# An own list scheduler orders all engines of a two-layer diffusion backbone, in place of the framework's order with hints

## The chip, the core and the metric

The kernel runs on one NeuronCore of a Trainium2 chip: TensorE (PE, matrix products), VectorE (DVE), ScalarE (ACT), GpSimd (POOL) and SyncE (SP), which issues most of the DMAs. Each engine works through its own list of instructions in order and waits on semaphores for the others. The metric is the device time of one execution in microseconds (us), the median of several.

## The reference, cut to what matters

The input is 256 latent tokens (`x`) and 256 context tokens (`ctx`), 1024 wide; there are two layers. All arithmetic is float32.

```python
for layer in range(2):
    mx = silu(c) @ w_ada[layer] + b_ada[layer]          # nine shift/scale/gate vectors, latent
    mc = silu(c_ctx) @ w_ada[layer] + b_ada[layer]      # the same for the context
    x  = x + 0.5 * mx[2] * swiglu(pre_norm(x, nw[0], mx, 0), ffn_up[layer, 0], ffn_down[layer, 0])
    ...                                                 # the context likewise
    yc, yx = token_mix(pre_norm(xc, ...), pre_norm(x, ...), ...)
    x  = x + mx[5] * yx
    x  = x + 0.5 * mx[8] * swiglu(pre_norm(x, nw[2], mx, 2), ffn_up[layer, 1], ffn_down[layer, 1])
return rms_norm(x, final_norm)
```

`pre_norm` is an RMS norm with a shift and a scale per channel. `swiglu` is 1024 to 2 x 2816 to 1024. `token_mix` projects the normalised tokens once (`w_in`), runs four bidirectional mixers (gated DeltaNet, Hyena, Mamba-2 SSD, gated linear attention) over chunks of 64 tokens, gates and merges them, and projects back (`w_out`).

## The kernel before, in words

**Dense work.** Activations lie transposed, 128 channels by 512 tokens a tile. A weight matrix comes in chunks of 128x1024 floats (512 KB): SP loads one into a `raw` tile (three buffers), POOL rounds it to fp32r (`wh`, L248; in part of the mixers ACT does, L245), DVE subtracts for the rest (`wl`, L249; or POOL, L246). PE takes three matmuls per tile to get float32 accuracy: `wh` x `hh` (L294), `wl` x `hh` (L295), `wh` x `hl` (L296); in the start L401 to L403 do this, for a projection by tokens L791 to L793. `wh` and `wl` have three buffers each, so a split waits until PE has done with the chunk three before.

**Norms.** `rstd_tok` sums squares on PE (L608), DVE makes the reciprocal root in a chain of eleven tiny instructions (`ms` L611, then `rq`, `rt`, `ru`, L210 to L215), PE broadcasts it (L623), DVE multiplies (`u`, L632), ACT and POOL apply scale and shift (`hh` L657, `v` L658), DVE takes the difference (`hl`, L659).

**adaLN vectors.** `ada` (from L508) multiplies `w_ada` by the condition on DVE in 1024 instructions (`aa`, L528 and L530) on loads `aw` of 256 KB. `pump` strews them under the dense work of the FFNs. The two vectors that the first norm needs are made on PE in `start` (L377).

**Mixers.** `weave` (L1964) runs two generators against each other: `chain`, the recurrent work of the mixers (many small instructions that go back and forth between PE, DVE, ACT and POOL, such as the triangular inverse `XA`, `Y`, `A` at L1092 to L1120), and `dense`, the projections. Tuned numbers (`PACE`) set how they interleave.

**What sets the order.** `start` is emitted under `manual_schedule`, so it runs in the order of the source; `norm_G` does this for PE. All the rest is ordered by the framework's scheduler, which is steered by hints: `issue_after` (a split or a load may not go before a named instruction; `gate`, `last_ld`), `high_priority` (weight splits get an offset), and the interleaving above. Tiles of one tag rotate through its buffers.

## Time and profile before

| what | value |
|---|---|
| median of 3 runs | 2842.53 us (2841.36 to 2853.82) |
| the profiled execution | 2847.14 us |
| its span, first to last instruction | 2845.2 us |
| PE busy | 2689.9 us, 95% |
| DVE, POOL, ACT busy | 2036.7 (72%), 1038.9 (37%), 529.4 us (19%) |
| mean granted TensorE clock | 0.978 of full speed |
| DMA | 382.66 MB, mean 134 GB/s |

The profiled execution is 4.6 us above the median; 1.9 us of it lie outside the span. The program goes through these stretches: start and first part of the first FFN (0 to 72 us), rest of that FFN (to 468), mixers of layer 0 (to 1209), output projection, second FFN and first FFN of layer 1 (to 2060), mixers of layer 1 (to 2634), last FFN for the latent tokens alone and output.

### The profile page before, as it was taken

The page shows a single profiled execution, that of the slowest core. Times are in us where ns is not written, and L with a number is a line of the kernel's source. Part 1 is how long each engine was busy: PE and PEld are TensorE (multiplying, and loading weights), DVE is VectorE, ACT ScalarE, POOL GpSimd, SP SyncE. Part 2 cuts the span into 40 slices and gives each one's busy share as a digit, 9 for nine tenths or more (in the row PEclk, how much of TensorE's full clock was granted, in tenths as well). Part 3 has the DMA queues.
Part 4 walks back from the last instruction along what each step waited for, and adds up shares of the span by engine and source line. Part 5 has one row for each costly group of instructions (what it writes and reads, how often), then busy time and mean ns, then how long its engine had stood idle before and what let it go on. Part 6 is the DMA issues. An engine that isn't in the chain of part 4 may idle for free. (4 is left out here: it accounts for less than half of the span.)

```text
span 2845.2 us, 40232 instructions
## 1 busy us (share of the span) xinstructions
PE 2689.9 (95%) x15131; PEld 2289.9 (80%) x15131; DVE 2036.7 (72%) x3763; ACT 529.4 (19%) x1044; POOL 1038.9 (37%) x1007
## 2 busy tenths in 40 slices
PE   7999999989999999999999999999987899989998
PEld 5777767778888878877778877788877798889998
DVE  5999875699575564459965469966479877778656
ACT  2000012533224231111000020000042322311100
POOL 4333313221332554535322233322244233455443
PEclk8999999999999999999999999999999999999999
DMA  9556534322434233234644336543333344445554
GB/s 273 168 178 198 174 109 132 89 75 71 141 112 131 77 100 101 85 116 145 180 145 130 102 110 181 176 146 117 95 89 108 96 138 133 143 150 186 154 185 142
DMA packets 369697, 382.66 MB, mean 134 GB/s; under 512 B 43466, under 2 KB 317544, under 8 KB 369504
## 3 DMA queue, kind: packets, MB, share of 16 engines
q1 hardware_dynamic: 347568, 363.67, 42.7%
q10 hardware_dynamic: 21936, 16.44, 1.8%
q8 instruction: 119, 1.95, 0.3%
q14 instruction: 74, 0.61, 0.1%
HBM read 355.79 MB, written 24.25 MB: 134 GB/s over the span
## 5 line engine op out<-in xcount | busy, mean ns | idle before, releaser
L248 POOL TENSOR_SCALAR wh<-raw 128x1024 fp32r<-128x1024 f32 (+1 forms) x460 | 570.7, 1241 | 1181.7 <-PE pmm L296 716.5
L294 PE MATMUL pmm<-hh,wh 128*128 128x512 f32 (+1 forms) x2432 | 887.0, 365 | 14.8 <-ACT raw L964 8.7
L295 PE MATMUL pmm<-hh,wl 128*128 128x512 f32 (+1 forms) x2432 | 880.7, 362 | 18.8 <-DVE wl L249 18.8
L296 PE MATMUL pmm<-hl,wh 128*128 128x512 f32 (+1 forms) x2432 | 878.8, 362 | 6.3 <-DVE hl L659 6.3
L249 DVE TENSOR_TENSOR wl<-raw,wh 128x1024 fp32r<-128x1024 f32 (+1 forms) x460 | 581.8, 1266 | 388.4 <-POOL wh L248 387.7
L295 PEld LDWEIGHTS pmm<-hh,wl 128*128 128x128 f32 x2432 | 467.6, 192 | 91.1 <-DVE wl L249 26.1
L294 PEld LDWEIGHTS pmm<-hh,wh 128*128 128x128 f32 x2432 | 467.5, 192 | 86.7 <-issue 15.4
L296 PEld LDWEIGHTS pmm<-hl,wh 128*128 128x128 f32 x2432 | 467.0, 192 | 76.2 <-DVE hl L659 10.6
L530 DVE SCALAR_TENSOR_TENSOR aa<-aw,cond,aa 128x256 f32<-128x256 f32 x896 | 423.9, 534 | 0.5 <-DMA aw<-in_w_ada 0.5
L295 PE MATMUL pmm<-ah,wl 128*128 128x512 f32 (+1 forms) x704 | 256.6, 364 | 1.6 <-DVE wl L249 1.4
L294 PE MATMUL pmm<-ah,wh 128*128 128x512 f32 (+1 forms) x704 | 258.0, 366 | 0.0
L296 PE MATMUL pmm<-al,wh 128*128 128x512 f32 (+1 forms) x704 | 256.5, 364 | 0.0
L682 ACT ACTIVATE sil<-pmm 128x512 f32<-128x512 f32 (+1 forms) x88 | 48.0, 545 | 812.2 <-PE pmm L296 773.3
L257 POOL TENSOR_SCALAR ah<-sil 128x512 fp32r<-128x512 f32 (+1 forms) x88 | 71.5, 813 | 251.5 <-DVE sil L687 228.8
L295 PEld LDWEIGHTS pmm<-ah,wl 128*128 128x128 f32 x704 | 133.2, 189 | 23.9 <-DVE wl L249 3.3
L294 PEld LDWEIGHTS pmm<-ah,wh 128*128 128x128 f32 x704 | 133.3, 189 | 23.2 <-issue 2.0
L296 PEld LDWEIGHTS pmm<-al,wh 128*128 128x128 f32 x704 | 133.3, 189 | 21.5 <-issue 0.8
L793 PE MATMUL pmm<-wl,hh 128*128 128x256 f32 x416 | 120.1, 289 | 6.3 <-DVE wl L249 6.3
L791 PE MATMUL pmm<-wh,hh 128*128 128x256 f32 x416 | 120.8, 290 | 0.0
L792 PE MATMUL pmm<-wh,hl 128*128 128x256 f32 x416 | 119.6, 288 | 0.0
L260 DVE TENSOR_TENSOR al<-sil,ah 128x512 fp32r<-128x512 f32 (+1 forms) x88 | 93.0, 1057 | 18.4 <-POOL ah L257 18.4
L296 PE MATMUL pmm<-yl,wh 128*128 128x512 f32 (+1 forms) x256 | 86.5, 338 | 1.3 <-DVE yl L260 1.3
(435 smaller groups left out, 3667.3 us busy)
## 6 DMA issues: line engine op xcount, KB each, us to landing
raw<-in_ffn_up SPq DMA_DIRECT2D x172, 512.0 KB
raw<-in_w_in SPq DMA_DIRECT2D x164, 512.0 KB
aw<-in_w_ada SPq DMA_DIRECT2D x288, 256.0 KB
raw<-in_ffn_down SPq DMA_DIRECT2D x80, 512.0 KB
raw<-in_w_branch SPq DMA_DIRECT2D x32, 512.0 KB
fe<-pk SPq DMA_DIRECT2D x42, 256.0 KB
raw<-in_w_out SPq DMA_DIRECT2D x16, 512.0 KB
pk<-pj ACTq DMA_DIRECT2D x26, 256.0 KB
```

Source lines behind the costliest of these rows:

```text
L248: nc.gpsimd.tensor_scalar(h, r, 1.0, 1.0, op0=ALU.mult, op1=ALU.mult)
L249: nc.vector.tensor_tensor(l, r, h.bitcast(F32), op=ALU.subtract)
L257: nc.gpsimd.tensor_scalar(hi, x, 1.0, 1.0, op0=ALU.mult, op1=ALU.mult)
L260: nc.vector.tensor_tensor(lo, x, hi.bitcast(F32), op=ALU.subtract)
L294: nc.tensor.matmul(o, h[:, k, js], rh[:, tj:t1], start=st, stop=False)
L295: nc.tensor.matmul(o, l[:, k, js], rh[:, tj:t1], start=False, stop=False)
L296: self.last_mm = nc.tensor.matmul(o, h[:, k, js], rl[:, tj:t1], start=False, stop=sp)
L530: nc.vector.scalar_tensor_tensor(a, x, c, a, op0=ALU.mult, op1=ALU.add)
L682: self.last_act = nc.scalar.activation(s[:, t0:t1], ps, AF.Silu)
L791: nc.tensor.matmul(o, rh[:, ts], h[:, k, :], start=st, stop=False, skip_group_check=True)
L792: nc.tensor.matmul(o, rl[:, ts], h[:, k, :], start=False, stop=False, skip_group_check=True)
L793: self.last_mm = nc.tensor.matmul(o, rh[:, ts], l[:, k, :], start=False, stop=sp, skip_group_check=True)
```

## The change

The body of the kernel is left as it is, but it is first run on a stand-in (`Stand`) which only notes each instruction: its engine, operands, the instructions that it depends on (by the overlap of rectangles of a tile, `box`), a cost by formulas (`cost`), and a key, which is the PE time noted so far. `Plan` then places all instructions of the five engines, SP's loads included, by a greedy simulation: whenever an engine is free, it takes of its ready instructions the one with the lowest key. An instruction counts as ready 150 ns (`margin`) and a latency after an instruction of another engine that it needs. Each tag's buffers are given out in the same pass. `build` emits the real instructions in that order under `manual_schedule` for all engines, each buffer as a tile of its own. The hints `issue_after`, `high_priority` and `manual_schedule` do nothing on the stand-in. Two tags get a buffer more (`adas` 1 to 2, `rows` 2 to 3). The instructions themselves stay the same, but for ACT's table loads, 31 before and 36 now.

```diff
+class Stand:
...
+    @contextlib.contextmanager
+    def issue_after(self, ins):
+        yield
...
+    def box(self, ap):
+        off, dims = ap.offset, list(ap.ap)
+        row = int(np.prod(self.tiles[ap.tensor.name][3][1:]))
+        p0, f0 = off // row, off % row
+        lo = hi = f0
+        for s, n in dims[1:]:
+            if s < 0:
+                lo += s * (n - 1)
+            else:
+                hi += s * (n - 1)
+        return p0, p0 + dims[0][1], lo, hi + 1
...
+        self.cost(o, aps)
+        o.key = self.t - self.off[-1]
+        if eng == "PE":
+            self.t += o.occ / 1e3
...
+    def cost(self, o, aps):
...
+        if o.dma:
+            o.occ, o.dur = (60.0 if o.eng == "SP" else 600.0), None
...
+            o.dur = 4.0 * n
+            return
...
+        elif o.eng == "DVE":
+            if o.name in ("tensor_scalar", "tensor_copy", "memset") and not ps and not r:
+                o.dur = 190 + 0.6 * E if o.name != "memset" else 100 + 0.5 * E
+            elif o.name == "scalar_tensor_tensor":
+                o.dur = max(150 + 1.045 * E, 250 + 0.87 * E) if E > 32 else 165
...
+            else:
+                o.dur = 150 + 1.06 * E
+            o.occ = o.dur - 70
...
+class Plan:
+    LAT = {"PE": 60, "DVE": 60, "ACT": 60, "POOL": 90, "SP": 90}
...
+                if e == "ACT":
+                    ta = table_of(o)
+                    if ta and ta != table:
+                        k += self.swap
+                if best is None or k < best[0]:
+                    best = k, n, c
...
+            if o.dma:
+                b = max(t + occ, dmaf)
+                dmaf = b + dur / 230.0
+                end = dmaf + 2300
+            else:
+                end = t + dur
...
+                elif x.eng == e and not o.dma:
+                    r = end if e != "PE" else t + occ
+                else:
+                    r = end + self.LAT[x.eng] + self.margin
...
+def build(nc, tc, es, st, plan):
...
+        return pools[pn].tile(list(shape), dtype, name=tn, tag=f"{tag}_{plan.slot[tn]}", bufs=1)
...
+    for n in plan.seq:
+        o = st.ops[n]
...
+        getattr(engines[o.eng], o.name)(*[sub(a) for a in o.args], **{k: sub(v) for k, v in o.kw.items()})
...
-            s = self.pt.tile([128, 256], F32, name=self.nm("adas"), tag="adas", bufs=1)
+            s = self.pt.tile([128, 256], F32, name=self.nm("adas"), tag="adas", bufs=2)
...
-        t = self.pt.tile([128, 128], F32, name=self.nm("rows"), tag="rows", bufs=2)
+        t = self.pt.tile([128, 128], F32, name=self.nm("rows"), tag="rows", bufs=3)
...
+def order(st):
+    plan = Plan(st, {}, 150.0, 8.0)
...
-    with _tile.TileContext(nc) as tc:
-        body(nc, tc, I, O)
+    st = Stand(nc)
+    body(st, st, I, O)
+    plan = order(st)
+    with _tile.TileContext(nc) as tc, contextlib.ExitStack() as es:
+        with tc.manual_schedule(engines=set(ENGINES)):
+            build(nc, tc, es, st, plan)
```

**The order at three places.** The number behind a tile's name is counted anew by each program; the first number (`raw22`, `ms52`) is the same in both. In the changed kernel every instruction has the line of `build` (L567).

Place 1, the start. On SP, the first loads after the inputs, before: `raw` are the first up-projection weights (a first and a second half, x2), `aw18` to `aw111` the `w_ada` blocks of the first norm, `aw153` onward those of the later vectors, `Fm` and `win` constants of the Hyena filter.

```order
L348 DMA aw21_131<-in_w_ada 128x4x128
L348 DMA raw22_136<-in_ffn_up 128x2x256 x2
L348 DMA aw23_139<-in_w_ada 128x4x128
...
L348 DMA raw31_155<-in_ffn_up 128x2x256 x2
L348 DMA raw71_338<-in_ffn_up 128x2x256 x2
L1641 DMA Fm0_1109<-in_dftF 128x512
...
L348 DMA aw63_322<-in_w_ada 128x4x128
...
L2012 DMA grp_80<-in_grp 128x10
L2013 DMA cmats_79<-in_cmats 128x9x128
...
L516 DMA aw153_789<-in_w_ada 128x512
```

And now:

```order
L567 DMA aw21_102<-in_w_ada 128x4x128
...
L567 DMA aw30_120<-in_w_ada 128x4x128
L567 DMA raw22_126<-in_ffn_up 128x2x256
L567 DMA raw31_128<-in_ffn_up 128x2x256
...
L567 DMA raw71_146<-in_ffn_up 128x2x256
L567 DMA grp_149<-in_grp 128x10
L567 DMA cmats_98<-in_cmats 128x9x128
L567 DMA aw153_152<-in_w_ada 128x512
...
L567 DMA aw170_161<-in_w_ada 128x512
L567 DMA Fm0_166<-in_dftF 128x512
...
L567 DMA aw70_264<-in_w_ada 128x4x128
...
L567 DMA raw22_126<-in_ffn_up 128x2x256
L567 DMA raw31_128<-in_ffn_up 128x2x256
L567 DMA raw71_146<-in_ffn_up 128x2x256
```

The second halves of the three first weight chunks have moved from right behind the first halves to behind `cmats`, five later `w_ada` blocks and the filter's constants. DVE, at the first norm, before (`ms` to `rq` is the root, `u` the product):

```order
L339 TENSOR_TENSOR acc32_159<-acc32_159,sq42_204 128x512
L339 TENSOR_TENSOR acc32_159<-acc32_159,sq46_222 128x512
L611 TENSOR_SCALAR ms52_263<-px51_254 128x4
L210 TENSOR_SCALAR rq53_265<-ms52_263 128x4
L213 TENSOR_TENSOR rt54_266<-ms52_263,rq53_265 128x4
...
L215 SCALAR_TENSOR_TENSOR rq53_265<-ru55_268,rq53_265 128x4
L389 TENSOR_REDUCE c00_299<-px49_235 128x4
...
L632 TENSOR_TENSOR u59_308<-x1_85,px58_303 128x512
L632 TENSOR_TENSOR u60_310<-x2_86,px58_303 128x512
L368 TENSOR_TENSOR wl62_313<-raw22_136,wh61_312 128x1024
```

And now:

```order
L567 COPY x7_286<-px45_278 128x512
L567 TENSOR_TENSOR acc32_242<-acc32_242,sq46_299 128x512
L567 COPY cond17_80<-cond2_320 128x8x2
L567 TENSOR_SCALAR aa157_331<-aw153_152,cond2_320 128x256
...
L567 SCALAR_TENSOR_TENSOR aa157_331<-aw155_156,cond2_320,aa157_331 128x256
...
L567 SCALAR_TENSOR_TENSOR aa163_362<-aw156_159,cond2_320,aa163_362 128x256
L567 TENSOR_SCALAR ms52_417<-px51_324 128x4
L567 SCALAR_TENSOR_TENSOR aa160_369<-aw156_159,cond2_320,aa160_369 128x256
L567 TENSOR_SCALAR rq53_424<-ms52_417 128x4
...
L567 SCALAR_TENSOR_TENSOR aa162_347<-aw170_161,cond2_320,aa162_347 128x256
L567 TENSOR_TENSOR wl62_493<-raw22_126,wh61_462 128x1024
L567 TENSOR_TENSOR u59_508<-x1_233,px58_489 128x512
```

Sixteen `aa` on `aw153` to `aw156`, which stood behind the whole start, now stand ahead of or between the first links of the root (14 of them ahead), and `wl62`, which needs the second half of `raw22`, ahead of the first `u`.

Place 2, the norm before the second FFN of layer 0 (`norm_G(0, 2)`), on DVE, before:

```order
L249 TENSOR_TENSOR wl2210_11287<-raw2208_11284,wh2209_11286 128x1024
L611 TENSOR_SCALAR ms2148_11083<-px2147_11074 128x4
L210 TENSOR_SCALAR rq2149_11085<-ms2148_11083 128x4
L213 TENSOR_TENSOR rt2150_11086<-ms2148_11083,rq2149_11085 128x4
L214 SCALAR_TENSOR_TENSOR ru2151_11088<-rt2150_11086,rq2149_11085 128x4
L1706 COPY gn2153_11101<-px2152_11098 1x256
L215 SCALAR_TENSOR_TENSOR rq2149_11085<-ru2151_11088,rq2149_11085 128x4
...
L214 SCALAR_TENSOR_TENSOR ru2151_11088<-rt2150_11086,rq2149_11085 128x4
L215 SCALAR_TENSOR_TENSOR rq2149_11085<-ru2151_11088,rq2149_11085 128x4
L1710 MEMSET gB2145_11064 1x256
L632 TENSOR_TENSOR u2156_11117<-x2092_10774,px2155_11112 128x512
```

And now:

```order
L567 TENSOR_SCALAR ms2148_11301<-px2147_11279 128x4
L567 SCALAR_TENSOR_TENSOR aa2314_11200<-aw2334_11202,cond2_320,aa2314_11200 128x256
L567 TENSOR_SCALAR rq2149_11308<-ms2148_11301 128x4
L567 SCALAR_TENSOR_TENSOR aa2318_11205<-aw2334_11202,cond2_320,aa2318_11205 128x256
L567 TENSOR_TENSOR rt2150_11312<-ms2148_11301,rq2149_11308 128x4
L567 COPY gn2153_11314<-px2152_11297 1x256
L567 SCALAR_TENSOR_TENSOR ru2151_11317<-rt2150_11312,rq2149_11308 128x4
L567 SCALAR_TENSOR_TENSOR aa2315_11208<-aw2334_11202,cond2_320,aa2315_11208 128x256
...
L567 SCALAR_TENSOR_TENSOR ru2151_11317<-rt2150_11312,rq2149_11308 128x4
L567 SCALAR_TENSOR_TENSOR aa2321_11228<-aw2335_11219,cond2_320,aa2321_11228 128x256
L567 SCALAR_TENSOR_TENSOR rq2149_11308<-ru2151_11317,rq2149_11308 128x4
L567 SCALAR_TENSOR_TENSOR aa2314_11200<-aw2347_11234,cond2_320,aa2314_11200 128x256
L567 SCALAR_TENSOR_TENSOR aa2318_11205<-aw2347_11234,cond2_320,aa2318_11205 128x256
```

Eight `aa` now stand between the eleven links of the chain, and five more between its end and the first `u`.

Place 3, the triangular inverse of the gated DeltaNet in layer 0, on PE, before (`px1031` is the first product of the inverse, `pmm` are dense):

```order
L296 MATMUL pmm1074_5479<-hl777_4098,wh1071_5462 128x512
L294 MATMUL pmm1073_5466<-hh780_4107,wh1088_5559 128x512
L1104 MATMUL px1031_5229<-XA1025_5198,MC902_4628 128x128 x4
L295 MATMUL pmm1073_5466<-hh780_4107,wl1089_5560 128x512
L296 MATMUL pmm1073_5466<-hl781_4108,wh1088_5559 128x512
```

And now:

```order
L567 MATMUL pmm1074_5344<-hl777_4224,wh1071_5219 128x512
L567 MATMUL pmm1073_5321<-hh780_4207,wh1088_5323 128x512
L567 MATMUL pmm1073_5321<-hh780_4207,wl1089_5334 128x512
...
L567 MATMUL pmm1074_5344<-hh786_4234,wl1089_5334 128x512
L567 MATMUL pmm1074_5344<-hl787_4256,wh1088_5323 128x512
L567 MATMUL px1031_5408<-XA1025_317,MC902_4715 128x128 x4
L567 MATMUL pmm1074_5344<-hh789_4245,wh1088_5323 128x512
L567 MATMUL pmm1074_5344<-hh789_4245,wl1089_5334 128x512
L567 MATMUL px1048_5426<-XA1042_3964,MC912_4774 128x128 x4
```

The first product stood behind one dense matmul of the chunk `wh1088` and now stands behind 21. Its producer on DVE, before (`XA1025` is its operand, `qkv` a convolution):

```order
L249 TENSOR_TENSOR wl1089_5560<-raw1087_5557,wh1088_5559 128x1024
L887 SCALAR_TENSOR_TENSOR qkv1016_5155<-raw1017_5156,vB0_3279,qkv1016_5155 128x2x254
L887 SCALAR_TENSOR_TENSOR qkv1018_5176<-raw1019_5177,vB0_3279,qkv1018_5176 128x2x254
...
L887 SCALAR_TENSOR_TENSOR qkv1018_5176<-raw1019_5177,vB0_3279,qkv1018_5176 128x2x254
L1079 STREAM_TRANSPOSE X0T1022_5191<-X01020_5187 128x512
L1080 STREAM_TRANSPOSE X11023_5192<-X1T1021_5188 128x512
L1082 TENSOR_TENSOR XC1024_5195<-X0T1022_5191,X1T1021_5188 128x512
L1092 COPY XA1025_5198<-X01020_5187 32x4x32
L1083 TENSOR_TENSOR XC1024_5195<-XC1024_5195,cmats_79 128x512
L1092 COPY XA1025_5198<-X01020_5187 32x4x32
```

And now:

```order
L567 TENSOR_TENSOR X939_262<-X939_262,P1012_5300 128x31
L567 SCALAR_TENSOR_TENSOR qkv1018_5302<-raw1019_5224,vB0_1399,qkv1018_5302 128x2x254
L567 SCALAR_TENSOR_TENSOR qkv1018_5302<-raw1019_5224,vB0_1399,qkv1018_5302 128x2x255 x2
L567 SCALAR_TENSOR_TENSOR qkv1018_5302<-raw1019_5224,vB0_1399,qkv1018_5302 128x2x254
L567 TENSOR_TENSOR wl1089_5334<-raw1087_5198,wh1088_5323 128x1024
L567 COPY XA1025_317<-X01020_5340 32x4x32 x2
L567 COPY A81027_406<-X01020_5340 32x4x32
L567 STREAM_TRANSPOSE X0T1022_5372<-X01020_5340 128x512
```

The copies of `XA1025` have moved ahead of the transposes and of `XC`, and no convolution stands between them and `wl1089` any more: four stand just ahead of `wl1089`, four further ahead.

## Rows read from the trace of the kernel before

**Rows 1.** Page, part 1: busy us, share of the span, instructions.

```profile
PE 2689.9 (95%) x15131; PEld 2289.9 (80%) x15131; DVE 2036.7 (72%) x3763; ACT 529.4 (19%) x1044; POOL 1038.9 (37%) x1007
```

**Rows 2.** Windows, six stretches: us, engines' busy us, granted clock, DMA share, GB/s.

```profile
0.00:72.00 72.00, 54.24 (x426) 40.86 (x427) 37.19 (x88) 20.41 (x40) 28.53 (x34) 0.83 0.96 271
72.00:468.00 396.00, 381.97 (x1734) 303.86 (x1732) 343.61 (x663) 29.44 (x52) 121.23 (x87) 0.98 0.55 165
468.00:1209.00 741.00, 710.50 (x3978) 605.63 (x3978) 479.82 (x939) 232.37 (x452) 293.41 (x295) 0.99 0.33 98
1209.00:2060.00 851.00, 828.30 (x3726) 669.04 (x3725) 591.98 (x1025) 72.05 (x126) 265.70 (x237) 0.99 0.46 137
2060.00:2634.00 574.00, 516.05 (x3654) 473.06 (x3652) 455.65 (x870) 156.07 (x333) 241.01 (x260) 0.96 0.44 130
2634.00:2845.20 211.20, 198.84 (x1621) 197.44 (x1621) 128.41 (x182) 19.03 (x42) 89.06 (x96) 0.97 0.51 160
```

**Rows 3.** Windows: a full stretch of the mixers, and 8 us behind a wait.

```profile
1067.00:1138.00 71.00, 71.00 (x333) 59.73 (x332) 31.22 (x45) 14.05 (x31) 34.45 (x32) 1.00 0.34 101
613.00:621.00 8.00, 8.00 (x40) 7.49 (x41) 5.40 (x15) 2.66 (x10) 1.93 (x5) 0.65 0.21 66
```

**Rows 4.** Waits of PE: line and releaser, us in total, times, longest us.

```profile
PE pmm L295 <- DVE wl L249: 20.2, 18, 3.2
PE px L1104 <- DVE XA L1092: 10.4, 3, 6.5
PE px L1626 <- ACT hyh L1596: 6.4, 1, 6.4
```

**Rows 5.** Timeline of DVE and PE, mixers of layer 0: start us, us, instruction.

```profile
603.63 6.29 DVE L887 SCALAR_TENSOR_TENSOR qkv<-raw,vB,qkv 128x510 f32<-128x510 f32 x5
612.47 0.22 DVE L1092 COPY XA<-X 32x128 f32<-32x128 f32 x1
612.83 2.04 PE L1104 MATMUL px<-XA,MC 128*128 128x128 f32 x8 [6.45 <-DVE XA L1092]
```

**Rows 6.** Timeline of DVE and PE in the start.

```profile
18.57 0.16 DVE L611 TENSOR_SCALAR ms<-px 128x4 f32<-128x4 f32 x1 [2.37 <-PE px L608]
24.93 0.50 PE L401 MATMUL pmm<-hh,wh 128*128 128x512 f32 x1
71.62 0.39 PE L403 MATMUL pmm<-hl,wh 128*128 128x512 f32 x1
```

**Rows 7.** Windows, 71 us each, of the FFNs.

```profile
71.00:142.00 71.00, 68.62 (x306) 55.32 (x305) 69.03 (x125) 4.30 (x8) 27.92 (x18) 0.98 0.57 167
142.00:213.00 71.00, 67.84 (x302) 53.87 (x301) 69.95 (x139) 3.20 (x6) 24.15 (x18) 0.98 0.59 178
1351.00:1422.00 71.00, 67.17 (x298) 53.48 (x297) 69.75 (x128) 3.98 (x7) 21.38 (x17) 0.98 0.60 178
```

**Rows 8.** Timeline of DVE and PE at the norm before the second FFN.

```profile
1278.93 0.16 DVE L611 TENSOR_SCALAR ms<-px 128x4 f32<-128x4 f32 x1 [1.05 <-PE px L608]
1281.39 0.16 DVE L215 SCALAR_TENSOR_TENSOR rq<-ru,rq 128x4 f32<-128x4 f32 x1
1282.86 2.48 DVE L632 TENSOR_TENSOR u<-x,px 128x512 f32<-128x512 f32 x4
1284.82 0.47 PE L294 MATMUL pmm<-hh,wh 128*128 128x512 f32 x1 [2.00 <-POOL v L658]
```

**Rows 9.** Timeline of ACT, its first table load.

```profile
3.88 1.28 ACT L489 ACT_TABLE_LOAD   x1 [3.88 <-DMA crow<-in_c]
```

**Rows 10.** Page, part 5: busy us, mean ns, idle before us.

```profile
L530 DVE SCALAR_TENSOR_TENSOR aa<-aw,cond,aa 128x256 f32<-128x256 f32 x896 | 423.9, 534 | 0.5 <-DMA aw<-in_w_ada 0.5
L260 DVE TENSOR_TENSOR al<-sil,ah 128x512 fp32r<-128x512 f32 (+1 forms) x88 | 93.0, 1057 | 18.4 <-POOL ah L257 18.4
```

**Rows 11.** Timeline of POOL and DVE in the first FFN.

```profile
101.69 1.05 POOL L248 TENSOR_SCALAR wh<-raw 128x1024 fp32r<-128x1024 f32 x1
101.76 1.52 DVE L260 TENSOR_TENSOR al<-sil,ah 128x512 fp32r<-128x512 f32 x1 [0.51 <-POOL ah L257]
```

More of the change, by code (lines that the diff above doesn't have):

```diff
@@ L1 @@
+import contextlib
+import heapq
 import math
@@ new lines, in build, with tile, sub @@
+def build(nc, tc, es, st, plan):
+    pools, real = {}, {}
+    engines = {"PE": nc.tensor, "DVE": nc.vector, "ACT": nc.scalar, "POOL": nc.gpsimd, "SP": nc.sync}
+    def tile(tn):
+        (pn, tag), bufs, pool, shape, dtype = st.tiles[tn][:5]
+        if pn not in pools:
+            kw = {"space": pool.space} if pool.space is not None else {}
+            pools[pn] = es.enter_context(tc.tile_pool(name=pn, bufs=1, **kw))
+        return pools[pn].tile(list(shape), dtype, name=tn, tag=f"{tag}_{plan.slot[tn]}", bufs=1)
+    def sub(x):
+        if not isinstance(x, bass.AP) or x.tensor.name not in st.tiles:
+            return x
+        tn = x.tensor.name
+        if tn not in real:
+            real[tn] = tile(tn)
+        b = real[tn]
+        if b.dtype != x.dtype:
+            b = b.bitcast(x.dtype)
+        return bass.AP(b.tensor, x.offset, [list(d) for d in x.ap])
+    table = None
+    left = {n: t[5] for n, t in st.tiles.items()}
+    for n in plan.seq:
+        o = st.ops[n]
+        if o.eng == "ACT":
+            ta = table_of(o)
+            if ta and ta != table:
+                nc.scalar.preload_act_table_set('natural_log_exp_and_others' if ta == "E" else 'silu_and_others')
+                table = ta
+        getattr(engines[o.eng], o.name)(*[sub(a) for a in o.args], **{k: sub(v) for k, v in o.kw.items()})
+        for tn in o.tiles:
+            left[tn] -= 1
+            if not left[tn]:
+                del real[tn]
@@ L469, in load_small @@
         nc, I = self.nc, self.I
-        t = self.pt.tile([128, 128], F32, name="crow", tag="rows", bufs=2)
+        t = self.pt.tile([128, 128], F32, name="crow", tag="rows", bufs=3)
         nc.scalar.dma_start(t[0:8, :], I["c_ctx"].rearrange("(k p) -> k p", p=128))
@@ L536, in ada @@
                                          start=st == 0, stop=st == 1, tile_position=(0, 32 * g))
-                s = self.pt.tile([128, 256], F32, name=self.nm("adas"), tag="adas", bufs=1)
+                s = self.pt.tile([128, 256], F32, name=self.nm("adas"), tag="adas", bufs=2)
                 nc.scalar.activation(s, ps[:, :256], AF.Copy)
@@ L2001, in mixers @@
         self.out_proj(l, t0, prep)
+ENGINES = [mybir.EngineType.PE, mybir.EngineType.DVE, mybir.EngineType.Activation, mybir.EngineType.Pool, mybir.EngineType.SP]
+def order(st):
+    plan = Plan(st, {}, 150.0, 8.0)
+    if plan.stuck:
+        raise RuntimeError("no order found")
+    return plan
 def body(nc, tc, I, O):
```

301 lines of the change are left out of this document (added).

## The prediction

> **What bounds the kernel now.** I read the page first: PE is busy 95% of the span, DVE 72%, POOL 37%, ACT 19% [rows 1]. So PE bounds the kernel, and since the change takes no instruction away, it can only win what PE loses: time in which PE stands, and time in which it runs at the lower clock. The windows by stretch give both [rows 2]. Idle time is the length less PE's busy time: 17.8 us in the start, 14.0 in the rest of the first FFN, 30.5 in the mixers of layer 0, 22.7 in the three parts up to 2060, 58.0 in the mixers of layer 1, 12.4 at the end; together 155 us. The clock has two levels, 2.4 and 1.2 GHz; a stretch with a mean of c loses about (1 - c) times its length: 12, 8, 7, 9, 23 and 6 us, together 65 and at most that, since idle time at the low clock counts in both. So some 220 us are to be had at the very most, and the start's 30 are not of the kind that an order can take away, as its DMA share is 0.96 at 271 GB/s. That PE can run without loss is seen in the mixers themselves, where 71 us hold 333 matmuls, 71.00 us busy, clock 1.00 [rows 3].
>
> The waits tell whom PE waits for [rows 4]: mostly DVE, in many short waits for `wl` (18, at most 3.2 us) and in few long ones for a link of a recurrence. One timeline shows the pattern [rows 5]: DVE works through five `qkv` convolutions (6.29 us) and makes `XA` afterwards, at 612.47; the product that needs it stands at a fixed place in PE's list, PE arrives 6.45 us early, and the dense matmuls queued behind it wait too. Then the clock is low: 0.65 over the next 8 us [rows 3], another 2.8 us. It is what an order that knows both lists could avoid: put the product later, or its producer earlier.
>
> **The change, part by part** (sums against the profiled execution's 2847.1 us, 1.9 of it outside the span; the median lies 4.6 lower).
>
> *The mixers, the main gain.* At the place shown, the product now stands behind 20 more dense matmuls, at 71.00/333 = 0.213 us worth 4.3 us of PE work, and DVE makes `XA` ahead of the transposes and of `XC` that it followed. In the trace the first transpose begins at the end of the convolutions, 603.63 + 6.29 = 609.9, and `XA` at 612.5 [rows 5], so that is some 2 us more. 4.3 and 2 cover nearly all of the 6.45 us. In both mixers together, PE idles 30.5 + 58.0 = 88.5 us and loses up to 30 to the clock [rows 2], 119 in all. Ends: nothing, if each wait is replaced by one of its kind; about 95, if four in five go. I take half, 59. I don't take more because the new order brings waits of its own: between some neighbouring `wl` of the mixers DVE now has more work than the three chunks ahead of it cover (a chunk of a projection is 24 matmuls, 5 us at 0.213), and the recurrences stay serial.
>
> *The FFNs' DVE-bound pieces.* From 71 to 213 us DVE is busy 69.0 and 70.0 of 71 us, and PE idles 2.4 and 3.2 us and loses up to 2.8 to the clock: 8.4 us; in 1351 to 1422 it is 3.8 and 1.4 [rows 7]. DVE is full there because of `aa`. In the new order `aa` run earlier, many in the start (37.2 of 72 us busy) and under the output projection. I take 6 in the first FFN and 10 in the later two, which have a piece of this kind each: 16. Ends: 4 and 22.
>
> *Hyena's hidden layer.* One wait of 6.4 us in the first FFN for `hyh` [rows 4], with about 2.8 of clock behind it as above. Its chain now stands some ten chunks earlier, so both go: 9 (ends 6 and 9). The cover is the FFN's dense work.
>
> *The start, a loss.* Before, the root of the first norm starts at 18.57 and the first dense matmul at 24.93; the last of the start ends at about 72 [rows 6]. Now 14 `aa` on `aw153` to `aw156` stand ahead of `ms52` on DVE, so all the norm waits until SP's loads down to `aw156` are there. Counted off SP's list they are 2 MB of inputs, 4.75 MB of first `w_ada` blocks, 0.75 MB of first halves, 0.6 of `cmats` and 1 MB of later blocks, about 9.1 MB: at 271 GB/s [rows 2], 34 us, and with the 5 us before the first load some 38. The first `u` also waits for `wl62`, whose second half comes 2 MB later, 46 us. So the first dense matmul comes about 22 us late. It isn't all lost: between 24.93 and 71.6 PE is paced by the loads, and as PE is busy 54.2 of 72 us at a mean clock of 0.83, its work behind the norm would need about 30 us at full clock, which gives an end near 80, and 9 us lost. The loads that were moved ahead are needed anyway, and the `aa` done early are in the term above. Ends: 4 (the later weights then wait for nothing) and 16 (the last half of the fourth weight chunk now comes behind 18 MB, 18/0.271 = 66 us, with 12 us of matmuls behind it, and DVE late). ACT's 27 small loads ahead of its first instruction cost nothing here: DVE waits for `aw156` longer.
>
> *Two norms, a loss.* Before the second FFN, and likewise before the first of layer 1, eight `aa` now stand between the links of the root and five behind it. The chain takes 2.6 us now, from 1278.93 to the end of `rq` at 1281.55, and DVE has 1.3 us until the first `u`; PE then stands 2.00 us [rows 8]. Eight times 0.534 [rows 10] is 4.3, and five less the gap of 1.3 is 1.4 more: 5.7 us a norm, during which PE has nothing but a few filter products. Two norms: 12 with a little low clock (ends 6 and 16).
>
> *Table loads.* Five more at 1.28 us [rows 9] on an engine that is busy 19%: 0; uncovered, they would be 6.
>
> *The rest of the edits* (buffers of `adas` and `rows`, other tile places): no row shows a wait that they would end; 0.
>
> *Durations that the order was made with.* The plan costs an `aa` at 473 ns and an `al` at 693 ns by its formulas; the trace has 534 and 1057 in the mean [rows 10]. One of these is seen in full: POOL's `wh` runs from 101.69 to 102.74, DVE's `al` starts at 101.76 and takes 1.52 us, ending about a normal `al` after POOL is done [rows 11]. The two kinds alone come to 896 x 61 + 88 x 364 ns = 87 us of DVE work that the plan doesn't know of. The Trainium skill, page "SBUF — State Buffer", section "SBUF: two separate sides", states why: a DVE operation with two SBUF inputs and a GpSimd operation that reads SBUF lock one shared pair of ports, and the loser is blocked until the other's instruction is over; the trace agrees at the place shown. By that rule the order is too tight wherever the plan runs a split on POOL beside DVE, and the sum would be the slower rival's below instead of mine.
>
> Sum: -59 - 16 - 9 + 9 + 12 = -63; 2847.1 - 63 = 2784 for an execution like the profiled one, 4.6 less for the median: **2780 us**.
>
> **The rivals.**
> *Larger gain:* the mixers lose only a fifth of what they lose now (-95) the start costs 4 and the norms 8: 2842.5 - 95 - 16 - 9 + 4 + 8, about 2735. For it: PE does run full for 71 us in the mixers. Against: the recurrences of layer 1, where only the latent half is projected and dense work is scarcer (58 us idle in 574).
>
> *No change:* the mixers' waits move to other places, gain 0: 2842.5 - 16 - 9 + 9 + 12 = 2838. For it: `wl` is already the most frequent wait, and the bursts of DVE between two `wl` grow.
>
> *Slower: DVE is late against the plan.* The place is the FFNs, where DVE is busy 344 of 396 us. DVE takes its list in order, so each `wl` behind an `aa` that the plan thought shorter, or whose load is later than in its model (60 ns an issue, 230 GB/s, no limit on loads in flight), is late, and with it PE. Price: the 87 us above, of which the share that DVE is short, some 35 of 87 (in the pieces of 71 us at 70 busy, DVE has under 2% of room, elsewhere a third), becomes PE's waiting; with the start at 16, the norms at 16 and the mixers gaining only 20: 2842.5 + 35 + 16 + 16 - 20 - 9 = 2880. It decides from the point where DVE's backlog passes the three `wl` buffers, 5 us a chunk, 15 us. Against it: the same `aa` at the same durations cost only some 24 us in the order of before, and they are now spread wider.
>
> *The change doesn't do what it says:* excluded as to the order, since the list of the built program shows it; what may fail is the clock, if the low stretches stay although the waits are shorter. That is within the no-change case.
>
> **How the numbers follow.** Forecast 0.55, larger gain 0.17, no change 0.10, slower 0.18. The forecast's own ends are 2842.5 + (-95 - 22 - 9 + 4 + 6) = 2727 and, with the mixers at 20, 2842.5 + (-20 - 4 - 6 + 16 + 16) = 2845; most of it lies between 2745 and 2815. For 8 in 10 the range takes in most of the larger gain and of no change, and stops short of the slower case's centre: 2722 to 2858. A measurement of this kernel can tell about 0.5% from no change, 14 us. Faster by more than that: the larger gain and nearly all of the forecast, 0.71; within it, 0.10; slower, 0.19.
>
> **What would show it.** The mixers' windows: PE idle near 45 us instead of 88 and a clock of 0.98 or more in layer 1. `XA` gone from the waits of over 3 us. In the start, `ms` at 36 us or later and the first dense matmul between 44 and 52; the start's last at 76 to 88. At the second norm, about 7 us from `ms` to the last `rq`. In 71 to 213, DVE below 68 of 71 us. I am wrong if the mixers' idle stays above 75 us, if PE's waits for `wl` in the FFNs grow beyond 40 us, or if the start ends where it did.

## The result and the profile after

The changed kernel takes **2928.16 us** (median of 4 runs, 2926.16 to 2930.3) against 2846.36 for the kernel before beside it: a ratio of 1.0285 [1.0258, 1.0313], **slower by 82 us**. The forecast was 2780 us, in a range of 2722 to 2858, with a chance of 0.19 on slower. The profiled execution took 2930.3 us, 2928.5 of it the span, at a mean clock of 0.973.

The page of the changed kernel, part 1, answers to [rows 1]:

```profile
PE 2701.6 (92%) x15131; PEld 2291.1 (78%) x15131; DVE 2041.0 (70%) x3763; ACT 536.5 (18%) x1049; POOL 1058.0 (36%) x1007
```

Apart from ACT's five table loads, the instructions are the same in number. PE's busy time grew by 11.7 us (its mean clock fell from 0.978 to 0.973), its idle time from 155.3 to 226.9 us, so by 71.6; the two make up the 83.3 us by which the span grew. So the loss is not more work: PE waits more. The windows of the changed kernel, cut where the stretches end in it (columns as in [rows 2]):

```profile
0.00:98.00 98.00, 52.57 (x430) 40.03 (x431) 47.80 (x114) 24.59 (x45) 30.97 (x44) 0.90 0.76 216
98.00:535.00 437.00, 396.11 (x1766) 311.26 (x1765) 331.07 (x655) 28.90 (x54) 121.03 (x94) 0.97 0.49 150
535.00:1262.90 727.90, 705.41 (x3944) 600.20 (x3943) 492.28 (x928) 232.26 (x449) 297.19 (x291) 0.99 0.33 97
1262.90:2147.80 884.90, 835.54 (x3721) 671.72 (x3721) 578.70 (x1020) 67.69 (x122) 264.56 (x239) 0.98 0.43 132
2147.80:2716.50 568.70, 513.55 (x3655) 470.47 (x3653) 467.19 (x869) 165.49 (x339) 248.25 (x246) 0.96 0.44 131
2716.50:2928.50 212.00, 198.44 (x1622) 197.44 (x1621) 124.00 (x183) 17.53 (x41) 95.98 (x96) 0.96 0.51 161
```

To compare stretch by stretch, the same PE instruction was looked up on either side of each boundary (0, 72, 475, 1209, 1290, 1636, 1707, 2060, 2634 us of the kernel before). Differences of length, in us (good to 1 or 2 us where the order around a boundary differs), with the forecast's term and those of two experiments that come below (e1, and e9, the best version):

| stretch | forecast | changed | e1 | e9 |
|---|---|---|---|---|
| start | +9 | +25.9 | +24.0 | -4.0 |
| first FFN (with hyena's hidden layer) | -15 | **+34.0** | +0.5 | -6.2 |
| mixers, layer 0 and 1 | -59 | -6.1, -4.3 | -16.4, -13.0 | -15.4, -15.1 |
| output projection and norm; norm of layer 1 | +12 | **+18.3, +18.5** | +9.8, +5.0 | +0.1, +3.0 |
| later FFNs (three) | -10 | -5.2, +2.3, -0.5 | -14.5, -9.7, -0.9 | -16.1, -10.2, +0.1 |

Two kinds of wait are new. **The first is in the FFNs.** PE's waits in the changed kernel (columns as in [rows 4]):

```profile
PE pmm L567 <- DVE sil L567: 33.2, 27, 2.3
PE px L567 <- ACT acc L567: 14.2, 1, 14.2
PE px L567 <- DVE Y L567: 12.5, 8, 3.7
PE px L567 <- DVE hl L567: 11.6, 3, 6.8
PE pmm L567 <- DVE wl L567: 9.3, 7, 3.5
```

`sil` was not among PE's waits before, and it isn't an operand of the matmul that waits: it is the multiplication on DVE that reads the old contents of a PSUM buffer. In the timeline of the first FFN it looks like this; first DVE, then PE:

```profile
191.71 5.23 DVE L567 SCALAR_TENSOR_TENSOR aa<-aw,cond,aa 128x256 f32<-128x256 f32 x11
196.85 1.21 DVE L567 TENSOR_TENSOR wl<-raw,wh 128x1024 fp32r<-128x1024 f32 x1
198.39 0.68 DVE L567 TENSOR_TENSOR sil<-sil,pmm 128x512 f32<-128x512 f32 x1
```

```profile
199.21 0.47 PE L567 MATMUL pmm<-hh,wh 128*128 128x512 f32 x1 [2.12 <-DVE sil L567]
```

The matmul starts a new accumulation, with operands that are long there. It was given the buffer that `sil` empties only at 198.39 + 0.68 = 199.07, and `sil` stands behind eleven `aa` and a split. Two more waits in PE's list are of this kind, for `gt` (6.9 us) and for `x` (6.6), which empty PSUM buffers too.

The built programs show whose buffer a tile gets. The accumulators `pmm` have four PSUM buffers. In the kernel before, the next user of a buffer is the fourth tile after the last one in 463 of 478 cases, so the buffers go round in turn; in the changed kernel it is the second tile after it in 309 cases, and the very next in 34.

**The second kind is at the norms.** Tile `gA`, a filter result that SP stores to DRAM, in the changed kernel: the stores, then who waited for the tile (us, times). Before, nobody waited for it.

```profile
L567 SPq DMA_DIRECT2D gdr<-gA x24: 283/366/9660, 441.6 to 2153.3; - x24
...
  DVE u L567: 22.1, 4
  ACT gA L567: 12.7, 1
  DVE gn L567: 10.9, 1
  PEld px L567: 6.8, 1
  DVE hSD L567: 6.5, 1
```

`u`, the product of the norm, reads nothing of `gA`. It was given a buffer of the same tag that `gA` has just left, and the last of the three stores of each `gA` lands only 13 to 18 us after SP begins to issue it (why, the last section tells). DVE and PE at the norm of layer 1:

```profile
1767.73 1.29 DVE L567 TENSOR_TENSOR u<-x,px 128x512 f32<-128x512 f32 x2 [7.19 <-DMA gdr<-gA]
```

```profile
1769.68 0.80 PE L567 MATMUL pmm<-hl,wh 128*128 128x512 f32 x1 [5.66 <-DVE hl L567]
```

The start lost 26 us in place of 9. ACT and DVE first, then PE:

```profile
22.14 1.28 ACT L567 ACT_TABLE_LOAD   x1 [22.14 <-DMA rows<-in_gdn_norm]
...
49.39 0.15 DVE L567 TENSOR_SCALAR ms<-px 128x4 f32<-128x4 f32 x1
...
59.78 2.05 DVE L567 TENSOR_TENSOR wl<-raw,wh 128x1024 fp32r<-128x1024 f32 x1 [6.35 <-POOL wh L567]
```

```profile
63.69 0.77 PE L567 MATMUL pmm<-hh,wh 128*128 128x512 f32 x1 [6.64 <-ACT hh L567]
```

The order of events is that of the forecast (`ms` behind the `aa`, the first `u` behind `wl62`, which waits for the second half of its weights), but `ms` comes at 49.4, far behind the 36 that was named as the earliest, and the first dense matmul at 63.7 where 44 to 52 was forecast.

### The profile page after: what moved, and what is told of

It is laid out like the page before. It is cut to its first block, busy times and chain, and to the rows that moved or that the text cites. A ratio compares the mean times of both kernels' runs of the same rounds, so it can differ in the third digit from the quotient of the medians.

```text
span 2928.5 us, 40340 instructions
## 1 busy us (share of the span) xinstructions
PE 2701.6 (92%) x15131; PEld 2291.1 (78%) x15131; DVE 2041.0 (70%) x3763; ACT 536.5 (18%) x1049; POOL 1058.0 (36%) x1007
## 4 chain that ended last, share of the span: by engine, by line
PE 58%; DVE 21%; issue 7%; POOL 6%; DMA 3%; ACT 1%; SPq 1%; DVEq 0%; POOLq 0%; ACTq 0%
PE pmm L567 49%; PE px L567 9%; DVE aa L567 7%; DVE wl L567 4%; POOL wh L567 3%; DMA gdr<-gA 2%; POOL v L567 1%; DVE qkv L567 1%; DMA gdr<-gn 1%; DVE X L567 1%; DVE P L567 1%; DVE sil L567 1%; SPq L567 1%; DVE xbc L567 1%; DVE al L567 0%
## 5 line engine op out<-in xcount | busy, mean ns | idle before, releaser
L567 POOL TENSOR_SCALAR wh<-raw 128x1024 fp32r<-128x1024 f32 (+1 forms) x466 | 592.3, 1272 | 1219.1 <-PE pmm L567 989.5
L567 PE MATMUL pmm<-hh,wh 128*128 128x512 f32 (+1 forms) x2464 | 904.7, 368 | 63.7 <-DVE sil L567 33.2
L567 PE MATMUL pmm<-hh,wl 128*128 128x512 f32 (+1 forms) x2464 | 893.5, 363 | 8.6 <-DVE wl L567 8.6
L567 DVE TENSOR_TENSOR wl<-raw,wh 128x1024 fp32r<-128x1024 f32 (+1 forms) x466 | 594.5, 1276 | 431.7 <-POOL wh L567 421.8
L567 PE MATMUL pmm<-hl,wh 128*128 128x512 f32 (+1 forms) x2464 | 888.6, 362 | 6.3 <-DVE hl L567 6.2
L567 PEld LDWEIGHTS pmm<-hh,wh 128*128 128x128 f32 x2464 | 473.4, 192 | 151.3 <-issue 49.3
L567 PEld LDWEIGHTS pmm<-hh,wl 128*128 128x128 f32 x2464 | 474.1, 192 | 75.9 <-DVE wl L567 10.6
L567 PEld LDWEIGHTS pmm<-hl,wh 128*128 128x128 f32 x2464 | 471.7, 192 | 78.2 <-DVE hl L567 9.1
L567 DVE SCALAR_TENSOR_TENSOR aa<-aw,cond,aa 128x256 f32<-128x256 f32 x896 | 428.0, 536 | 0.3 <-DVE ms L567 0.3
L567 PE MATMUL pmm<-ah,wh 128*128 128x512 f32 (+1 forms) x704 | 259.8, 369 | 8.3 <-DVE x L567 5.5
L567 PE MATMUL pmm<-ah,wl 128*128 128x512 f32 (+1 forms) x704 | 256.7, 365 | 0.0
L567 PE MATMUL pmm<-al,wh 128*128 128x512 f32 (+1 forms) x704 | 256.5, 364 | 0.0
L567 ACT ACTIVATE sil<-pmm 128x512 f32<-128x512 f32 (+1 forms) x88 | 48.0, 545 | 815.4 <-PE pmm L567 794.8
L567 PEld LDWEIGHTS pmm<-ah,wh 128*128 128x128 f32 x704 | 133.7, 190 | 35.0 <-issue 8.7
L567 PEld LDWEIGHTS pmm<-al,wh 128*128 128x128 f32 x704 | 133.5, 190 | 21.2
L567 PEld LDWEIGHTS pmm<-ah,wl 128*128 128x128 f32 x704 | 133.8, 190 | 20.5 <-issue 0.4
L567 POOL TENSOR_SCALAR ah<-sil 128x512 fp32r<-128x512 f32 (+1 forms) x88 | 69.0, 789 | 160.4 <-DVE sil L567 156.4
L567 PE MATMUL pmm<-wh,hh 128*128 128x256 f32 x416 | 119.9, 288 | 0.0
L567 PE MATMUL pmm<-wl,hh 128*128 128x256 f32 x416 | 119.1, 287 | 0.8 <-DVE wl L567 0.8
L567 PE MATMUL pmm<-wh,hl 128*128 128x256 f32 x416 | 118.6, 285 | 0.0
L567 PE MATMUL pmm<-yh,wh 128*128 128x512 f32 (+1 forms) x256 | 88.4, 346 | 3.3 <-DVE gt L567 3.2
L567 POOL TENSOR_SCALAR v<-u,Am,mods 128x256 f32<-128x256 f32 x72 | 56.3, 794 | 93.5 <-DVE u L567 74.4
```

Source lines behind the costliest of these rows:

```text
L567: getattr(engines[o.eng], o.name)(*[sub(a) for a in o.args], **{k: sub(v) for k, v in o.kw.items()})
```

## The experiments

**Theory A:** the plan hands out buffers badly. Of the buffers of a tag that are free at a moment of its simulation, it takes the one freed *last*, and it counts a buffer as free 60 ns after its last reader, without the margin that operands get. As long as the chip keeps the plan's times that costs nothing; a late reader makes the next writer wait. **Theory C**, the forecast's slower rival: DVE is late because its costs in the plan are too low. And the start may have been lost by the hints that the stand-in ignores. All edits are in the planner and its stand-in; what is computed stays the same. A "kernel before" beside each run took 2844 to 2848 us.

**e1, the oldest free buffer.** The order on every engine stays the same, in the built programs instruction for instruction (e7 likewise); only places differ (the small tiles of the pool `pt` are left as they were).

```diff
-                f = max((x for x in fr if x[0] <= t), key=lambda x: x[0])
+                f = (max if c[0] == "pt" else min)((x for x in fr if x[0] <= t), key=lambda x: x[0])
```

> Edit: the same plan and the same order on every engine, but a new tile takes the buffer that has been free longest instead of the one that came free last (the small tiles of one pool left as they are). Theory A (tight buffers: any lateness of the real chip against the plan turns into a wait for the previous user of a buffer that the plan had only just freed, worst where a slow 1 KB store still reads gA): the waits for the stores of gA and gn (DVE 33 us, ACT 13 us in the changed kernel) go, the PE idle at 424 to 456, 1338 to 1352 and 1747 to 1770 falls by 30 us or more, PE's 33 us of waits for the sil product shrink by half; total 2865 to 2895. Theory B (the hints that were dropped kept bulk work out of the way of the short chains): buffers are not the matter, total 2915 to 2930, first dense matmul still at 60 to 65. Theory C (wrong durations of DVE work): no change either.

Measured: **2832.55 us**, ratio to the kernel before 0.995 [0.9933, 0.9967]; 96 us less than the changed kernel, more than theory A asked, and against B and C, which expected no change. The waits of PE in e1:

```profile
PE pmm L567 <- DVE wl L567: 18.5, 16, 3.5
PE px L567 <- ACT acc L567: 12.5, 1, 12.5
PE px L567 <- DVE Y L567: 12.5, 8, 3.7
```

`sil`, `gt` and `x` are gone from PE's waits, and no `u` waits for a store any more. Accumulators go round in turn again (463 of 478). As the order is the same, instruction for instruction, giving each tile the oldest buffer takes away the whole loss and more.

**e7, the oldest buffer in PSUM alone** (`min` for PSUM's tags, `max` for all others).

> Edit: the changed kernel with the oldest buffer for PSUM tiles alone; SBUF tiles take the one freed last, as in the change. If the PSUM buffers behind the dense matmuls are the matter (the 33 us that PE waits for the sil product), the total falls by 35 to 50, to 2878 to 2893, and the waits for gA's stores stay. If the SBUF buffers are (gA, u, gn, hSD), it falls by under 25 and stays above 2903.

Measured: 2881.39 us, 1.0117 [1.0099, 1.0136]; 47 of the 96 us. `sil` is gone from PE's waits, and what is left is the other half, by the waits of all engines in e7:

```profile
DVE u L567 <- DMA gdr<-gA: 22.7, 4, 7.6
POOL v L567 <- DMA gdr<-gn: 19.5, 3, 7.5
```

The first FFN falls from +34.0 to +7.3, the norms stay at +18.7 and +17.6: each kind of wait is in its own place. The 47 us are what PE's waits for `sil`, `gt` and `x` came to, 46.7. Of the other 49, the norms have 21 (from e7 to e1 they fall by 8.9 and 12.6), the mixers another 21 and the first FFN 7, so the stores at the norms are about half of it.

**e14, the plan told of the slow stores** (the changed kernel; a buffer of `gA` or `gn` counts as free 15 us later).

```diff
-                    free[c2].append((endt[tn] + 60, self.slot[tn]))
+                    free[c2].append((endt[tn] + (15000 if tn[:2] in ("gA", "gn") else 60), self.slot[tn]))
```

> Edit: the change, but the plan frees the buffers of gA and gn 15 us after their last store is issued and landed by its model, so that none is handed on while the slow store still reads it; all else (last-freed buffers, costs, no hints) as in the change. If the SBUF half of the loss is these stores: 2880 to 2895, no more waits of u and v for gA and gn. If it is spread over many short waits for SBUF buffers: 2910 to 2930.

Measured: 2908.35 us, 1.0218 [1.0197, 1.0239]; 20 us less than the changed kernel, between the two expectations. The trace tells why it isn't more: `u` now gets the buffers of `gB`, the third tile that is stored, of which the plan was not told.

```profile
DVE u L567 <- DMA gdr<-gB: 21.8, 4, 6.4
```

So the 20 us are no measure of what the stores cost: taking the last freed buffer, the plan passed the wait on to the next tile that is stored.

**e10, DVE's costs alone** (the changed kernel, theory C by itself).

```diff
                 o.dur = 150 + 1.06 * E
+            o.dur *= 1.12
```

> Edit: the change as it is (last-freed buffers, no hints), with DVE costs 12% up alone. Theory A: with buffers given out so tightly, costs nearer to the chip make the plan less late, so part of the loss goes, but not the waits for gA's stores nor the start: 2885 to 2912. Theory C, as far as it claims to be the cause of the loss: under 2870. If lateness on DVE has nothing to do with the waits for buffers: 2920 to 2935.

Measured: 2867.4 us, 1.0074 [1.0059, 1.0089], 61 us less: theory C's expectation, and not theory A's 2885 to 2912. PE's waits for `sil` fall from 33.2 us to

```profile
PE pmm L568 <- DVE sil L568: 6.9, 17, 0.6
```

The buffers are as tight as in the changed kernel (the second tile after in 295 of 478 cases), so it is the lateness of DVE that went. It can be seen in the plan itself: by its formulas DVE is busy for 1788 us, in the trace for 2041, 14% more; times 1.12 the plan has 2034. **e13, e1 and these costs together** tells whether the two add up:

> Edit: the change with the oldest buffer (e1) and DVE costs 12% up (e10), no hints. If the two are one cause seen from two sides (DVE behind the plan, and buffers that turn this into waits), their gains overlap in the first FFN and the norms: 2805 to 2825. If they are independent, the gains of 96 and 61 add: 2765 to 2785.

Measured: 2804.55 us, 0.9856 [0.9838, 0.9873], 124 us less than the changed kernel, where 96 and 61 would be 157. That is just below the range for one cause seen from two sides, and far from the sum. So they overlap: one removes lateness, the other what turned it into a wait. The costs alone leave 63 us of the 124; the buffers alone leave 28.

**e2, the hints kept** (changed kernel; `issue_after` becomes a dependence in the plan), and **e3, e1 and e2 together.**

```diff
     def issue_after(self, ins):
+        self.hold.append(ins)
         yield
+        self.hold.pop()
...
+        for h in self.hold:
+            if h is not None:
+                o.deps.setdefault(h, -1)
```

> Edit: issue_after on the stand-in adds a dependency on the start of the named instruction, so that the hints of the body hold in the plan; buffers as in the change. Theory B: ACT's small loads and the later w_ada blocks move behind the start, first dense matmul at 35 to 48 instead of 63.7, the start's loss of 27 us against before falls to 5 to 15, and fewer adaLN products stand in the root chains; total 2890 to 2912. Theory A: the start improves but the waits for gA's stores stay at 40 us or more, total not below 2890.

> Edit: the oldest buffer and the hints together. If A and B are both causes and independent, the gains add: 2835 to 2870. If one hides the other, it stays near the better of the two alone.

Measured: e2 2907.39 us, 1.0209 [1.0194, 1.0224]; e3 2822.83 us, 0.9914 [0.99, 0.9929]. In both the start gives back about 20 us (first dense matmul at 46.2 and 46.0 us, start +3.1 in e3 against +24.0 in e1): the loads and splits that the hints held back had gone ahead of the norm. The gains of e1 and e2, 96 and 21, nearly add (105), so the hints are a cause beside the buffers, in the start.

**e4, both halves of a weight load free of each other** (e3, and two DMAs that write one tile don't depend on each other), **e5, the start by hand** (e4, and `manual_schedule` keeps the source's order on the engines that it names).

> Edit: as e3, and two DMAs that write one tile no longer wait for each other in the plan, so that the second halves of the first weight chunks stand right behind the first. Theory A and B: the first chunk's split no longer waits for the loads of everything else; first dense matmul at 24 to 32 and the start ends at 72 to 78, total 2820 to 2855, 8 to 25 below e3. If DVE's durations (theory C) are what is left, the FFN stretch 111 to 262 of the changed kernel keeps its 13 us of idle PE in all four.

> Edit: as e4, and manual_schedule on the stand-in keeps the order of the source on the engines that it names (the start on PE, DVE, ACT and POOL; the norms' filter products on PE). Theory B': what e4 still loses in the start (first dense matmul at 44.1 against 24.9 before) is the order among the first norm's own instructions, where a split that waits for its load stands ahead of the short chain: first dense matmul at 24 to 28, start's end at 71 to 76, total 2800 to 2815. Rival: the loads set the start's end anyway (0.96 of the DMA engines busy before), and e4 gained back 13 of its 19 us by 104 us; then total 2815 to 2825.

Measured: e4 2824.32 us, 0.9918 [0.9903, 0.9933], a miss: no gain, first dense matmul at 44.1. In its trace DVE takes two splits, which wait for their loads, ahead of the norm's first links:

```profile
24.69 3.18 DVE L573 TENSOR_TENSOR wl<-raw,wh 128x1024 fp32r<-128x1024 f32 x2 [5.85 <-POOL wh L573]
```

e5: 2813.29 us, 0.9884 [0.9869, 0.9899], first dense matmul at 28.0, as expected.

**e6, e8, e9: slack in the plan.** e6 is e5 with DVE's costs times 1.12, e8 is e5 with a margin of 400 ns for 150, e9 is both.

> Edit: as e5, and the plan costs every DVE instruction 12% longer, about what the trace shows over the formulas (aa 536 ns against 473, al 1057 against 693). Theory C: the plan stops overfilling DVE ahead of the splits, PE's waits for wl fall from 32 to 20 us or less, total 8 to 20 us below e5. Rival: the lateness on DVE is taken up by the three weight buffers, and greedy order doesn't change much: within 5 us of e5.

> Edit: as e5, with a margin of 400 ns in place of 150 behind each hand-over between engines. If lateness against the plan is still what makes PE wait, a larger margin puts consumers later and the total falls by 5 to 15. If the waits come from too much DVE work ahead of a split, the margin does nothing: within 5 us of e5.

> Edit: as e6 (oldest buffer, hints, both halves, order by hand in the start, DVE costs 12% up) with a margin of 400 ns in place of 150. e8 gained 10 over e5, nearly all of it in the mixers of layer 1, and e6 gained 22, 16 of it in the FFNs. If the two act in different places: 2778 to 2786. If both only make up for the same lateness of DVE: 2788 to 2794.

Measured: e6 2791.16 us, 0.9804 [0.9789, 0.9819]; e8 2803.3, 0.9845 [0.983, 0.986]; **e9 2782.76, 0.9778 [0.9763, 0.9792]**, the best of all, 63.8 us below the kernel before beside it. PE's waits for `wl` fall from 32.2 us in e5 to 10.4 in e6, so theory C holds there too. The windows of e9's first FFN, 71 us each, as in [rows 7]:

```profile
66.00:137.00 71.00, 71.00 (x324) 57.61 (x324) 67.70 (x120) 5.17 (x9) 29.84 (x20) 1.00 0.63 191
137.00:208.00 71.00, 71.00 (x324) 57.49 (x323) 70.05 (x137) 3.08 (x6) 30.14 (x19) 1.00 0.57 176
208.00:279.00 71.00, 71.00 (x336) 57.34 (x335) 70.05 (x136) 2.27 (x5) 21.35 (x15) 1.00 0.65 195
```

The like windows of the changed kernel:

```profile
98.00:169.00 71.00, 64.94 (x286) 51.62 (x285) 67.83 (x132) 4.40 (x8) 25.96 (x18) 0.98 0.59 180
169.00:240.00 71.00, 66.86 (x301) 52.51 (x300) 60.51 (x114) 2.78 (x5) 23.84 (x19) 1.00 0.51 154
240.00:311.00 71.00, 65.94 (x300) 52.81 (x299) 60.49 (x127) 2.00 (x4) 23.17 (x14) 1.00 0.56 175
```

In two of e9's windows DVE is as full as before (70.05 of 71 us), and PE stands in none; in the changed kernel DVE has 3 to 10 us of room in 71 and PE idles 4 to 6.

**Misses with e11, e12 and e15.** In e11 (e6, where a successor on the same engine is ready after the issue time and not the end) and e12 (e11 with the margin of 400), and e15 (e9 with e14's edit):

> Edit: as e6, and an instruction that follows another of its own engine counts as ready when the engine is free, not 70 ns later, so that nothing of lower rank slips in between two links of a chain on DVE. If the slipped-in instructions matter still: 5 to 15 us below e6, most in the mixers' triangular solves. If the hints have already taken them out: within 4 us of e6.

> Edit: as e11 with a margin of 400 ns. If e9 and e11 gain in different ways their gains add; the best of all, 2770 to 2785, is expected if so; otherwise it equals the better of the two within 4 us.

> Edit: e9 with the same 15 us for gA and gn. With the oldest buffer there is little left of it: within 4 us of e9 (2782.8); if the two waits of about 9 us that the oldest buffer left (gn, hSD) still stand in PE's way, 5 to 9 below.

Measured: e11 2807.49 us, 0.9862 [0.9846, 0.9879], 16 slower than e6; e12 2799.69, 0.9834 [0.9819, 0.9849]; e15 2788.28, 0.9799 [0.9782, 0.9816], 5.5 slower than e9. e11 loses in the mixers of layer 0 (+6.0 where e6 has -5.6); which rule of the plan brings that about was not found. A greedy order changes in many places after a small edit, so between two plans a difference under some 16 us can't be put down to the edit alone. The gains of e1, e7, e10 and e13 are three to eight times that, and in e1 and e7 the order did not change at all; that of e6 lies just above it, and so does that of e14, whose order differs in 22 places. Those of e3 over e1 (10), e5 over e4 (11), e8 over e5 (10) and e9 over e6 (8) lie below: that e9 is the best is measured, what its last steps gave is not.

## Why the prediction was wrong

**The step that failed** is "the rest of the edits (buffers of `adas` and `rows`, other tile places): no row shows a wait that they would end; 0". It asked which wait the new places would end, and not which they would start. Their price was 96 us (e1), 47 of it in PSUM (e7) and 49 in SBUF. The kernel before gave the buffers out in turn, so a buffer had rested for as long as its tag has buffers; DVE's lateness was hidden there, and no row of before could show it. The line of `Plan` that takes the `max` was part of the change and stood to be read. Without this step the sign would have been right and the gain still too large: with rotated buffers e1 is 14 us faster than the kernel before, where -63 was forecast. What is missing there lies in the start (+24 for +9), the first FFN (+0.5 for -15) and the mixers (-29 for -59); the later FFNs give more than forecast (-25 for -10).

**The slower rival had half of it.** DVE is late against the plan, as it said (e10 and e6 gain 61 and 22 us by dearer DVE), but its place was the three `wl` buffers, and PE's waits for `wl` fell, from 20.2 us [rows 4] to 9.3. Its point of decision, a backlog of 15 us, was wrong as well: with the buffer freed last there is no such cushion. And of its 87 us, the 32 at `al` did not come: `al` took 1057 ns in the mean before, and takes 664 now. (The plan's 693 holds for 66 of the 88; the rest are half as wide.)

```profile
L567 DVE TENSOR_TENSOR al<-sil,ah 128x512 fp32r<-128x512 f32 (+1 forms) x88 | 57.6, 664 | 14.5 <-POOL ah L567 14.4
```

Over all 88 the plan is 5 us short. `aa` was late as priced (536 ns for 473), and kinds that were not priced were late too, `wl` above all (575 us in the trace, 533 in the plan).

The Trainium skill, page "SBUF — State Buffer", section "SBUF: two separate sides", states that a DVE operation with two SBUF inputs and a GpSimd operation that reads SBUF block each other. The forecast gave it as the reason why `al` is dearer than planned; the trace of the changed kernel doesn't agree there (664 ns). No run separates the shared ports from other errors of the cost formulas.

**The start, +9, measured +25.9.** Two parts were too small. First, the loads that the `aa` need landed later than by the forecast's sum: DVE waits for them until 45.96 us, where the sum gave 38.

```profile
45.96 1.14 DVE L567 TENSOR_SCALAR aa<-aw,cond 128x256 f32<-128x256 f32 x4 [0.62 <-DMA aw<-in_w_ada]
```

SP's first twelve `w_ada` issues stretch over more time than in e4, where the hints hold all but five of ACT's small loads back. Here they are in the changed kernel, then in e4:

```profile
9.82 15.43 SPq L567 DMA_DIRECT2D aw<-in_w_ada  x12
```

```profile
6.83 9.85 SPq L573 DMA_DIRECT2D aw<-in_w_ada  x12
```

An issue itself is short (0.37 us in the median of the changed kernel's twelve); between them SP waits for earlier DMAs to land, small loads (`hyv`) among them, 15.4 us in the first 26:

```profile
SPq L567 <- DMA aw<-in_w_ada: 6.8, 6, 4.2
SPq L567 <- DMA hyv<-in_hy_b: 2.3, 1, 2.3
```

In the built program the DMAs of SP and ACT take eight completion semaphores in turn, and each waits until the DMA eight before it has landed, so that a small load of ACT counts for as much as 256 KB of SP. During the twelve issues the DMAs moved 161 GB/s, in e4 292; the forecast's sum by bytes took 271 [rows 2].

Second, "ACT's 27 small loads cost nothing" is false. They are among what SP waits for, and ACT's first activation, an `acc`, waits behind them until 23.4 us (in e4 it comes at 7.34), for which PE stands 14.2 us. So the sums that `ms` reads are done only at 40.2 us: even with no `aa` ahead of it `ms` would have come 21.6 us later than before.

The order that the forecast named (the norm behind the `aa`, and behind the second half of the weights) is in the trace; that the norm's own inputs would be nearly as late, it did not see. No run takes the small loads away alone.

**The norms, +12, measured +36.8.** The chain itself came out as forecast, 6.6 us for about 7. Behind it, `u` waits for the stores; that part is the failed step again.

```profile
1338.08 0.16 DVE L567 TENSOR_SCALAR ms<-px 128x4 f32<-128x4 f32 x1 [0.59 <-PE px L567]
1344.58 0.14 DVE L567 SCALAR_TENSOR_TENSOR rq<-ru,rq 128x4 f32<-128x4 f32 x1
1349.79 0.69 DVE L567 TENSOR_TENSOR u<-x,px 128x512 f32<-128x512 f32 x1 [3.08 <-DMA gdr<-gA]
```

With other buffers the two stretches are at +14.8 (e1), near the forecast, and with the hints too at +0.1 (e3).

**The mixers, -59, measured -10.4.** The wait that was shown went, as forecast: `XA` is not among PE's waits any more. But even with rotated buffers and slack, the mixers gain 29 to 31 us (e1, e9). Idle time there is 22.5 + 55.2 = 77.7 us in the changed kernel, above the 75 that was named as the sign of being wrong; the clock in layer 1 stayed at 0.96, where 0.98 was to show the gain. "Half of 119" was a share without a row behind it; about a quarter is what the runs gave, as in e9's mixers waits for `xbc` (8.4 us), `wl` (7.4) and `Y` (6.9) take the place of `XA`.

**The FFNs.** In the first, -15 became +34.0, by `sil`. In the later ones the forecast's -10 is outdone once the buffers rotate (-25.1 in e1). But the reading "DVE-bound" did not follow from DVE's busy time in these pieces: in e9 DVE is busy 70.05 us of 71 and PE 71.00. How much of that is a better order, and how much the fewer `aa` in e9's windows (94 and 90 in the first two, 101 and 96 before), no run separates.

Table loads at 0 stand unrefuted. That e9 ends at 2782.8, near the forecast's 2780, is no confirmation: start and FFNs gave what the mixers didn't.

## What to carry to other kernels

When a scheduler or an allocator replaces another, read how it picks among free buffers before costing anything else: here the one freed last turned lateness into waits of 96 us, which the one freed first absorbed, at the same order and with the same number of buffers. A wait for something that isn't an operand (`pmm` for `sil`, `u` for the store of `gA`) is the mark of a reused buffer. And compare a plan's costs with the trace in sum: 14% too little for DVE was worth 61 us with tight buffers and 28 with rotated ones (e10, and e13 against e1). Whether slack beyond the true costs helps isn't shown; the larger margin's 8 to 10 us lie within what any small edit moves.
